# A differential-attention block on one core: the first row tile's scores as two matmuls of 256 columns instead of four of 128, with the sum of the two partial products moved from the matmul accumulator to VectorE

## The chip, the core and the metric

The kernel runs on one core of a Trainium2 chip. The engines named below are TensorE (PE in the profile; PEld is its weight load), VectorE (DVE), ScalarE (ACT) and GpSimd (POOL); SP is a queue that only starts transfers. The metric is the time of one execution on the device, in microseconds. Before the change three runs gave a median of 676.17 us (675.97 to 676.85).

## The reference, cut to what matters

One layer over 512 tokens of width 1024. A combined projection gives q, k, v, a pooling input and two gates; differential attention and a causal pooling branch are gated, summed and projected; a squared-ReLU MLP follows. The change touches only the scores of the attention, computed for 8 heads, each with two components c of 64 dimensions, and in four blocks of 128 query rows:

```python
for i in range(S // Q_BLOCK):                 # 4 blocks of 128 rows
    q0 = i * Q_BLOCK
    kend = q0 + Q_BLOCK                       # block i sees the first (i+1)*128 keys
    qb = q[:, q0:kend]
    kb = k[:, :kend]
    vb = v[:, :kend]
    s = jnp.einsum('bqhcd,bkhcd->bhcqk', qb, kb).astype(jnp.float32)
    mask = jnp.arange(kend)[None, :] <= (q0 + jnp.arange(Q_BLOCK))[:, None]
    s = jnp.where(mask, s, -jnp.inf)
    p = jax.nn.softmax(s, axis=-1)
    w = p[:, :, 0] - lam * p[:, :, 1]
    outs.append(jnp.einsum('bhqk,bkhd->bqhd', w.astype(v.dtype), vb))
```

All of it is float32. The kernel keeps that precision by splitting each operand into a high part, rounded to the matmul's own type, and a low part, the remainder.

## The kernel before, in words

**Stages.** First the value projection (v); then the attention stage, in which the projections of q and k, the scores, the pooling and the gates of all heads are mixed; then the output projection (po); then the MLP with its up and down products (um, dm).

**One head.** `qk(h)` projects q and k, applies the rotation on VectorE (`rope`, lines 349 to 353) and splits the results. For component c the 64 dimensions of q stand twice in the 128 partitions of `qs[:, c]`: the high part on the component's own half, the low part on the other. `kz[:, c]` has the high part of k on the own half and zeros on the other, `ks[:, c]` has the low part on the own half and the high part on the other. So `qs*ks` gives high times low plus low times high, `qs*kz` gives high times high, and the two sum to the score. `kz` are two fixed tiles, `ks` comes from a pool of two. Lines 379, 381 and 382 (ScalarE, ScalarE, VectorE) write them.

**The scores.** `attn(h)` goes over the four row tiles i with N = (i+1)*128 keys. For each component it takes one of two PSUM banks (3 and 4, in turn) and runs two matmuls into it, line 394 with `ks` and line 395 with `kz`, the second accumulating. VectorE's line 396 then adds the mask, scales, clips and takes the row extreme in one instruction. ScalarE's line 400 is the exponential with its row sum. Lines 402 to 405 normalize and combine the two components; line 409 transposes the result on TensorE (matmuls of 128 columns, i+1 of them for tile i); lines 411 and 412 split the transposed weights into `wt`; line 417 multiplies by the values.

**What sets the order.** The program is written head by head, with filler projections (gates `ga`, `gp` and pooling `u`) between heads by the table LAG. The framework then orders the instructions of every engine anew, by a timeline that it computes for itself at build time from its own costs. Each engine runs its list strictly in that order, so an instruction whose input is late holds all that stand behind it. A change of one operation can thus move many others.

**Other engines around it.** GpSimd adds for the pooling windows (line 452, after line 444 has made `u`), for the norm of the attention output (426, 427) and for the gated output (481), and starts accumulating transfers for low weight parts (line 122).

## Time and profile before

| | |
|---|---|
| median of the runs | 676.17 us |
| span of the profiled execution | 675.2 us |
| what the median has beside the span | 1.0 us |
| mean granted clock of TensorE | 0.998 |
| TensorE busy | 665.3 us, 99% |
| VectorE busy | 529.1 us, 78% |
| ScalarE busy | 462.5 us, 68% |
| GpSimd busy | 123.0 us, 18% |

The page gives the profiled execution's span, from its first to its last instruction, and no other time of it. A row of the timeline has the start of an instruction (or of a merged run of equal ones), its duration, engine, line, operation and its tiles, output before input. TensorE's rows overlap, since a matmul starts before the one ahead of it has drained; what a matmul costs in a dense stream is therefore read from the distance between starts, not from its duration. In a tile's name the buffer number is left out, so `s` is any score tile and `t` any transposed one.

### The profile page before, as it was taken

How to read it: one execution, taken by the hardware profiler on the slowest of the kernel's cores; microseconds unless marked ns; L12 is line 12 of the kernel's file. 1: busy time of each engine (PE TensorE's matmuls, PEld its weight loads, DVE VectorE, ACT ScalarE, POOL GpSimd, SP SyncE). 2: the span in 40 equal slices, each digit the busy share in tenths (PEclk: the TensorE clock that was granted, in tenths of full speed). 3: DMA queues.
4: the chain of work that ended last, by engine and by line, in shares of the span. 5: the costliest groups of instructions: out<-in, count | busy, mean ns of one | idle time of the engine just before them, and what ended most of it. 6: DMA issues, size and time to landing. Idle time of an engine off the chain costs nothing.

```text
span 675.2 us, 9995 instructions
## 1 busy us (share of the span) xinstructions
PE 665.3 (99%) x3686; PEld 579.9 (86%) x3686; DVE 529.1 (78%) x879; ACT 462.5 (68%) x741; POOL 123.0 (18%) x137
## 2 busy tenths in 40 slices
PE   9999999999999999999999999999999999999995
PEld 7788888888888888888889988899889998899884
DVE  6955877799979986975478989667994599747995
ACT  8465587978887698883477975367753696356874
POOL 6201110132133212520201020202103021210120
PEclk9999999999999999999999999999999999999999
DMA  8526574435254364574964678676969579493863
GB/s 272 189 71 182 126 152 125 102 94 126 87 139 105 101 171 94 126 193 177 309 194 79 196 172 241 153 179 155 234 190 197 200 156 260 125 213 131 213 125 124
DMA packets 32880, 109.34 MB, mean 162 GB/s; under 512 B 4032, under 2 KB 4928, under 8 KB 32832
## 3 DMA queue, kind: packets, MB, share of 16 engines
q0 software_dynamic: 10656, 38.80, 32.4%
q1 hardware_dynamic: 21744, 69.38, 29.0%
q8 instruction: 29, 0.48, 0.3%
q10 hardware_dynamic: 432, 0.52, 0.2%
q14 instruction: 19, 0.16, 0.1%
HBM read 106.59 MB, written 2.10 MB: 161 GB/s over the span
## 4 chain that ended last, share of the span: by engine, by line
PE 86%; DMA 5%; issue 5%; DVE 1%; ACT 1%; SPq 0%; DVEq 0%; POOLq 0%
PE dm L838 7%; PE dm L840 7%; PE dm L841 7%; PE um L759 7%; PE um L764 7%; PE um L761 7%; DMA wga_uNone<-w_up 5%; PE o L417 2%; PE ga L132 2%; PE ga L131 2%; PE gp L135 2%; PE k L132 2%; PE gp L132 2%; PE gp L131 2%; PE k L131 2%
## 5 line engine op out<-in xcount | busy, mean ns | idle before, releaser
L840 PE MATMUL dm<-wh_dt,z 128*128 128x512 f32 (+1 forms) x128 | 49.5, 387 | 0.0
L841 PE MATMUL dm<-wl_dt,z 128*128 128x512 f32 (+1 forms) x128 | 49.4, 386 | 0.0
L838 PE MATMUL dm<-wh_dt,z 128*128 128x512 f32 (+1 forms) x128 | 49.0, 387 | 0.0
L759 PE MATMUL um<-gss,wh_ut 128*128 128x256 f32 x192 | 48.1, 284 | 0.1
L761 PE MATMUL um<-gss,wh_ut 128*128 128x256 f32 x192 | 48.1, 283 | 0.0
L400 ACT ACTIVATE p<-p,st 128x128 f32<-128x128 f32 (+3 forms) x64 | 35.8, 560 | 14.1 <-DVE st L396 13.8
L112 ACT CAST wh_ut<-wga_uNone 128x1024 fp32r<-128x1024 f32 x24 | 24.9, 1053 | 28.8 <-PE dm L840 19.2
L856 DVE TENSOR_TENSOR x<-x,dm 128x512 f32<-128x512 f32 x48 | 32.8, 687 | 14.1 <-PE dm L841 14.0
L670 POOL DMA_DIRECT2D wga_dNone<-w_dn x16 | 14.2, 887 | 151.8 <-DVE wl_dt L113 151.8
L113 DVE TENSOR_TENSOR wl_ut<-wga_uNone,wh_ut 128x1024 fp32r<-128x1024 f32 x24 | 29.0, 1224 | 12.5 <-ACT wh_ut L112 12.5
L112 ACT CAST wh_ub<-wr_u 128x1024 fp32r<-128x1024 f32 x24 | 25.1, 1051 | 19.0 <-PE um L761 10.1
L670 POOL DMA_DIRECT2D wga_uNone<-w_up x18 | 15.6, 867 | 120.9 <-DVE wl_ut L113 86.9
L840 PE MATMUL dm<-wh_db,z 128*128 128x512 f32 x96 | 37.2, 389 | 0.0
L841 PE MATMUL dm<-wl_db,z 128*128 128x512 f32 x96 | 37.2, 389 | 0.0
L759 PEld LDWEIGHTS um<-gss,wh_ut 128*128 128x128 f32 x192 | 36.8, 192 | 0.3 <-ACT rawz L776 0.3
L761 PEld LDWEIGHTS um<-gss,wh_ut 128*128 128x128 f32 x192 | 36.9, 192 | 0.0
L838 PE MATMUL dm<-wh_db,z 128*128 128x512 f32 x96 | 35.8, 390 | 0.0
L113 DVE TENSOR_TENSOR wl_ub<-wr_u,wh_ub 128x1024 fp32r<-128x1024 f32 x24 | 29.2, 1222 | 7.9 <-ACT wh_ub L112 7.9
L112 ACT CAST wh_dt<-wga_dNone 128x1024 fp32r<-128x1024 f32 x24 | 24.8, 1050 | 14.6 <-issue 4.1
L735 DVE TENSOR_TENSOR z<-rawz,z 128x1024 fp32r<-128x1024 f32 x28 | 33.7, 1225 | 0.9 <-ACT z L732 0.9
L396 DVE CUSTOM_DVE_ANT_0 p<-s,mask 128x128 f32<-128x128 f32 (+3 forms) x64 | 30.3, 485 | 3.4 <-PE s L395 3.3
L732 ACT CAST z<-rawz 128x1024 fp32r<-128x1024 f32 x28 | 28.7, 1048 | 6.0 <-DVE rawz L741 4.9
(324 smaller groups left out, 2222.9 us busy)
## 6 DMA issues: line engine op xcount, KB each, us to landing
wr_u<-w_up SPq DMA_DIRECT2D x24, 512.0 KB, 5.3
wr_d<-w_dn SPq DMA_DIRECT2D x24, 512.0 KB, 4.2
wga_uNone<-w_up POOLq DMA_DIRECT2D x18, 512.0 KB, 6.7
wga_dNone<-w_dn POOLq DMA_DIRECT2D x16, 512.0 KB, 5.8
wr_k<-w_in SPq DMA_DIRECT2D x8, 512.0 KB, 3.3
wr_ga<-w_in SPq DMA_DIRECT2D x8, 512.0 KB, 3.3
wr_gp<-w_in SPq DMA_DIRECT2D x8, 512.0 KB, 4.2
wl_ga<-w_in POOLq DMA_DIRECT2D x8, 512.0 KB, 5.5
```

The source lines that it names most:

```text
L112: ins = A.copy(out=hi[:, sl], in_=raw[:, sl])
L113: (eng or G).tensor_tensor(out=lo[:, sl], in0=raw[:, sl], in1=f(hi)[:, sl], op=ALU.subtract)
L131: T.matmul(acc, lhsT=hi[:, c], rhs=rh[:, k, :], start=k == 0, stop=False)
L132: T.matmul(acc, lhsT=hi[:, c], rhs=rl[k], start=False, stop=False)
L400: A.activation(out=pr[:, c, :N], in_=pr[:, c, :N], func=AF.Exp, scale=-1.0, bias=st[:, c : c + 1], accum_out=st[:, 2 + c : 3 + c])
L735: V.tensor_tensor(out=z[:, 1], in0=r, in1=f(z[:, 0]), op=ALU.subtract)
L759: m = T.matmul(a_, lhsT=hi[:, c], rhs=rh[:, k, :], start=p + k == 0 and onto is None, stop=False, skip_group_check=True)
L761: T.matmul(a_, lhsT=hi[:, c], rhs=rl[:, k, :], start=False, stop=False, skip_group_check=True)
L764: m = T.matmul(a_, lhsT=lo[:, c], rhs=rh[:, k, :], start=False, stop=k == 3, skip_group_check=True)
L838: m = T.matmul(a_, lhsT=zh, rhs=hi[:, sl], start=p == 0 and start, stop=False, skip_group_check=True)
L840: T.matmul(a_, lhsT=zl, rhs=hi[:, sl], start=False, stop=False, skip_group_check=True)
L841: end = T.matmul(a_, lhsT=zh, rhs=lo[:, sl], start=False, stop=p == 3, skip_group_check=True)
```

## The change: what it does

The two copies of k, `ks` and `kz`, become two halves of one tile `kk` of shape 128 x 2 x 2 x 512 (copy, component, key). For the first row tile (i = 0, 128 keys) one matmul per component streams both copies, 2 x 128 columns, so that the two partial products land side by side in one PSUM bank; both components share that bank, 512 columns in all. VectorE then adds the mask to the first partial product of both components (a new instruction, 128 x 2 x 128) and writes it to `pr`; the instruction that adds the mask in the other row tiles here takes the second partial product and `pr` in the mask's place. Row tiles 1 to 3 are as before. The score banks are taken seven times per head, not eight.

```diff
--- before.py
+++ after.py
@@ -361,15 +361,14 @@
 
     lo_, hi_ = slice(0, 64), slice(64, 128)
 
-    kzs = [cf.tile([P, 2, S], F32R, name=f"kz{i}") for i in range(2)]
-    for kz in kzs:
-        G.memset(f(kz)[hi_, 0, :], 0.0)
-        G.memset(f(kz)[lo_, 1, :], 0.0)
+    kks = [cf.tile([P, 2, 2, S], F32R, name=f"kk{i}") for i in range(2)]
+    for kk in kks:
+        G.memset(f(kk)[hi_, 1, 0, :], 0.0)
+        G.memset(f(kk)[lo_, 1, 1, :], 0.0)
 
     def qk(h):
         qs = tp.tile([P, 2, S], F32R, tag="qs", name=f"qs{h}", bufs=2)
-        ks = tp.tile([P, 2, S], F32R, tag="ks", name=f"ks{h}", bufs=2)
-        kz = kzs[h % 2]
+        ks, kz = (kks[h % 2][:, i] for i in range(2))
         q = rope(proj(h, f"q{h}", V) if h else q0, f"q{h}")
         for c, own, oth in ((0, lo_, hi_), (1, hi_, lo_)):
             A.copy(out=qs[own, c, :], in_=q[own])
@@ -380,21 +379,31 @@
         for c, own, oth in ((0, lo_, hi_), (1, hi_, lo_)):
             A.copy(out=ks[oth, c, :], in_=f(kz)[own, c, :])
             V.tensor_tensor(out=ks[own, c, :], in0=k[own], in1=f(kz)[own, c, :], op=ALU.subtract)
-        return qs, ks, kz
-
-    def attn(h, qs, ks, kz):
+        return qs, kks[h % 2]
+
+    def attn(h, qs, kk):
+        ks, kz = (kk[:, i] for i in range(2))
         wt = wt_all
         for i in range(NT):
             N = (i + 1) * P
             qsl = slice(i * P, i * P + P)
             pr = tmp(f"p{i}", f"p{h}_{i}", (P, 2, N), bufs=1)
             st = tmp("st", f"st{h}_{i}", (P, 6), bufs=3)
+            if i == 0:
+
+                both = sbk(f"s{h}_0").rearrange("p (c k n) -> p c k n", c=2, k=2)
+                for c in range(2):
+                    T.matmul(both[:, c], lhsT=qs[:, c, qsl], rhs=kk[:, :, c, :P], start=c == 0, stop=True, skip_group_check=True)
+                diag = mask[:, S - P :].rearrange("p (o n) -> p o n", o=1).to_broadcast([P, 2, P])
+                V.tensor_tensor(out=pr, in0=both[:, :, 0], in1=diag, op=ALU.add)
             for c in range(2):
-                s_ = sbk(f"s{h}_{i}_{c}")
-                T.matmul(s_[:, :N], lhsT=qs[:, c, qsl], rhs=ks[:, c, :N], start=True, stop=False)
-                T.matmul(s_[:, :N], lhsT=qs[:, c, qsl], rhs=kz[:, c, :N], start=False, stop=True)
+                if i:
+                    s_ = sbk(f"s{h}_{i}_{c}")
+                    T.matmul(s_[:, :N], lhsT=qs[:, c, qsl], rhs=ks[:, c, :N], start=True, stop=False)
+                    T.matmul(s_[:, :N], lhsT=qs[:, c, qsl], rhs=kz[:, c, :N], start=False, stop=True)
                 V.tensor_tensor_reduce(
-                    out=pr[:, c, :N], in0=s_[:, :N], in1=mask[:, S - N :], scale=-0.125, scalar=-NEG,
+                    out=pr[:, c, :N], in0=s_[:, :N] if i else both[:, c, 1], in1=mask[:, S - N :] if i else pr[:, c],
+                    scale=-0.125, scalar=-NEG,
                     op0=ALU.add, op1=ALU.min, accum_out=st[:, c : c + 1],
                 )
                 A.activation(out=pr[:, c, :N], in_=pr[:, c, :N], func=AF.Exp, scale=-1.0,
```

In the changed kernel the score matmuls are lines 396 (first tile), 402 and 403; the new VectorE addition is line 398, the mask and extreme line 404, the combination line 414, the split of the transposed weights line 421; line 382 has become 381, line 444 line 453, line 435 line 444, line 409 line 418.

**The order on TensorE, head 0, first row tile.** In the rows, `s0_0` and `s0_1_0` are score tiles (head, row tile, component, then a buffer number), `ga0` a gate projection that runs between them. Before:

```order
L131 MATMUL ga0_893<-xh_84,wh_ga0_888 128x512
L394 MATMUL s0_0_0_635<-ks0_579,qs0_578 128x128
L395 MATMUL s0_0_0_635<-kz0_572,qs0_578 128x128
L132 MATMUL ga0_893<-xlb_86,wh_ga0_888 128x512
L394 MATMUL s0_0_1_640<-ks0_579,qs0_578 128x128
L395 MATMUL s0_0_1_640<-kz0_572,qs0_578 128x128
```

Now:

```order
L131 MATMUL ga0_889<-xh_84,wh_ga0_884 128x512
L396 MATMUL s0_0_634<-kk0_572,qs0_578 128x256
L402 MATMUL s0_1_0_652<-kk0_572,qs0_578 128x256
L403 MATMUL s0_1_0_652<-kk0_572,qs0_578 128x256
L396 MATMUL s0_0_634<-kk0_572,qs0_578 128x256
L132 MATMUL ga0_889<-xlb_86,wh_ga0_884 128x512
```

Four rows of 128 columns have become two of 256, and the first scores of row tile 1 stand between them.

**The order on VectorE, head 0, the same place.** `p0_0` and `p0_1` are the masked scores of row tiles 0 and 1, `st` their row extremes. Before:

```order
L353 TENSOR_TENSOR q1k1_824<-q1k1_824,swk1_826 128x512
L396 ISA p0_0_633,st0_0_634<-s0_0_0_635,mask_96 128x128
L396 ISA st0_0_634 128x1
L456 SCALAR_TENSOR_TENSOR pb0_873<-pa0_872,u0_869 128x512
L396 ISA p0_0_633,st0_0_634<-s0_0_1_640,mask_96 128x128
```

Now:

```order
L353 TENSOR_TENSOR q1k1_820<-q1k1_820,swk1_822 128x512
L398 TENSOR_TENSOR p0_0_632<-s0_0_634,mask_96 128x256
L465 SCALAR_TENSOR_TENSOR pb0_869<-pa0_868,u0_865 128x512
L404 ISA p0_0_632,st0_0_633<-s0_0_634,p0_0_632 128x128
L404 ISA st0_0_633 128x1
```

One addition of 256 elements per partition stands ahead of the two instructions that were there already.

**The order around the last transpose of head 4.** First VectorE, up to the combination `p4_3` that this transpose reads; `kk1` holds the k of head 5, `u2` starts the pooling adds of GpSimd, `o3` and `y3` belong to the output norm of head 3. Before (the combination of `p4_2`, row tile 2, stands eleven rows ahead of the first of these):

```order
L403 TENSOR_SCALAR st4_3_1915<-st4_3_1915,lvec_506 128x1
L444 TENSOR_TENSOR u2_2087<-u2_2062,rb_114 128x512
L435 SCALAR_TENSOR_TENSOR o3_1628<-o3_1628,con_73,y3_1639 128x512
L382 TENSOR_TENSOR ks5_1969<-q1k5_2042,kz1_573 64x512 x2
L405 SCALAR_TENSOR_TENSOR p4_3_1914<-p4_3_1914,st4_3_1915 128x512
```

Now:

```order
L414 SCALAR_TENSOR_TENSOR p4_2_1877<-p4_2_1877,st4_2_1878 128x384
L205 SCALAR_TENSOR_TENSOR sqo3_1621<-ss3_1624,sqo3_1621 128x512
L353 TENSOR_TENSOR q1k5_2026<-q1k5_2026,swk5_2028 128x512
L421 TENSOR_TENSOR wt_571<-t4_1_1872,wt_571 128x2x128
L411 RECIPROCAL st4_3_1900<-st4_3_1900 128x2
L453 TENSOR_TENSOR u2_2071<-u2_2046,rb_114 128x512
L206 SCALAR_TENSOR_TENSOR y3_1627<-sqo3_1621,y3_1627 128x512
L412 TENSOR_SCALAR st4_3_1900<-st4_3_1900,lvec_506 128x1
L381 TENSOR_TENSOR kk1_573<-q1k5_2026,kk1_573 64x512 x2
L444 SCALAR_TENSOR_TENSOR o3_1616<-o3_1616,con_73,y3_1627 128x512
L414 SCALAR_TENSOR_TENSOR p4_3_1899<-p4_3_1899,st4_3_1900 128x512
```

The two combinations have come nearer to each other, and `u2` now stands ahead of line 206. On TensorE the transposes `t4_2` and `t4_3` that read them have come nearer too. Before, 32 matmuls of 512 columns and two of 128 stood between them; now these rows, with seven matmuls of `ga4` and seven of `q6`, each of 512 columns, between `t4_2` and the first of them:

```order
L396 MATMUL s5_0_2127<-kk1_573,qs5_1953 128x256
L402 MATMUL s5_1_0_2145<-kk1_573,qs5_1953 128x256
L403 MATMUL s5_1_0_2145<-kk1_573,qs5_1953 128x256
L132 MATMUL q6_2247<-xla_85,wh_q6_2243 128x512
L396 MATMUL s5_0_2127<-kk1_573,qs5_1953 128x256
L131 MATMUL q6_2247<-xh_84,wh_q6_2243 128x512
```

Four more rows of `q6` follow, and then `t4_3`. Between the two transposes there are now 20 matmuls of 512 columns and four of 256. Past the attention stage the lists of all engines are as before, and SP's list is as before throughout.

## The prediction

> **What bounds the kernel now.** I read the page first, for the shares of the engines and the chain of work that ended last; then the waits of TensorE; then the busy time in four stretches of the attention stage, in which the change lies.
>
> ```profile
> PE 665.3 (99%) x3686; PEld 579.9 (86%) x3686; DVE 529.1 (78%) x879; ACT 462.5 (68%) x741; POOL 123.0 (18%) x137
> PE 86%; DMA 5%; issue 5%; DVE 1%; ACT 1%; SPq 0%; DVEq 0%; POOLq 0%
> ```
>
> ```profile
> PE h2T L629 <- ACT h2f L646: 0.6, 1, 0.6
> PE um L759 <- ACT gss L602: 0.3, 1, 0.3
> ```
>
> TensorE is busy for 99% of the span and makes up 86% of the chain. A busy row of TensorE includes its drain, so the share alone is no proof; but apart from the start, the waits that the profile finds for it are these two, both behind the attention stage, and two more of 0.3 us or less ahead of it. In the attention stage no matmul waits by this view. So time saved in TensorE's stream there is time saved at the end, unless another engine becomes late. VectorE is the next one:
>
> ```profile
> 166.00:194.00 28.00, 28.00 (x136) 23.36 (x136) 23.02 (x49) 22.81 (x38) 6.75 (x6) 1.00 0.45 113
> 194.00:222.00 28.00, 28.00 (x136) 23.18 (x135) 27.59 (x56) 21.43 (x44) 10.79 (x10) 1.00 0.38 102
> 222.00:253.00 31.00, 31.00 (x152) 26.00 (x151) 27.63 (x69) 24.17 (x50) 6.06 (x6) 1.00 0.52 131
> ```
>
> The columns are the stretch, its length, then the busy time of PE, PEld, DVE, ACT and POOL, the clock and the DMA share. VectorE has 5.0 us of idle time between 166 and 194 us (28.00 - 23.02) and 3.4 us between 222 and 253 us, but only 0.4 us between 194 and 222 us, where heads 4 and 5 meet. The granted clock is 1.00 in all, so a duration read in one place holds in another.
>
> **What the change takes from TensorE.** Eight heads times four matmuls of 128 columns go, eight times two of 256 come; the number of streamed columns is the same. What each costs is read from distances between starts (first the 128-column scores of head 0, then 256-column scores a little later):
>
> ```profile
> 81.71 0.39 PE L131 MATMUL ga<-xh,wh_ga 128*128 128x512 f32 x1
> 81.94 0.22 PE L394 MATMUL s<-ks,qs 128*128 128x128 f32 x1
> 82.00 0.27 PE L395 MATMUL s<-kz,qs 128*128 128x128 f32 x1
> 82.11 0.45 PE L132 MATMUL ga<-xlb,wh_ga 128*128 128x512 f32 x1
> 82.39 0.22 PE L394 MATMUL s<-ks,qs 128*128 128x128 f32 x1
> 82.45 0.28 PE L395 MATMUL s<-kz,qs 128*128 128x128 f32 x1
> 82.56 0.45 PE L131 MATMUL ga<-xh,wh_ga 128*128 128x512 f32 x1
> 82.85 0.40 PE L132 MATMUL ga<-xlb,wh_ga 128*128 128x512 f32 x1
> ```
>
> ```profile
> 86.95 0.39 PE L132 MATMUL q<-xla,wh_q 128*128 128x512 f32 x1
> 87.17 0.28 PE L394 MATMUL s<-ks,qs 128*128 128x256 f32 x1
> 87.29 0.28 PE L395 MATMUL s<-kz,qs 128*128 128x256 f32 x1
> 87.41 0.39 PE L131 MATMUL q<-xh,wh_q 128*128 128x512 f32 x1
> 87.64 0.28 PE L394 MATMUL s<-ks,qs 128*128 128x256 f32 x1
> 87.75 0.28 PE L395 MATMUL s<-kz,qs 128*128 128x256 f32 x1
> 87.87 0.39 PE L132 MATMUL q<-xla,wh_q 128*128 128x512 f32 x1
> ```
>
> A 512-column matmul stands 0.227 us ahead of its successor where eight follow one another (1.81 us for eight in the chain: "PE q L135 x8"):
>
> ```profile
> 61.93 1.81 PE q L135 x8
> 380.93 0.48 PE um L764 x4
> ```
>
> From 81.71 to 82.85 us lie three matmuls of 512 columns and four of 128: 1.14 - 3*0.227 = 0.46 us, or 0.115 us for each of 128 columns. From 86.95 to 87.87 us lie two of 512 and four of 256: 0.92 - 2*0.227 = 0.47 us, or 0.117 us for each of 256; the second row of the last fence gives 0.120. So a matmul of 128 columns costs as much as one of 256: halving the columns saves nothing, since each has its own load of weights. The gain is 32*0.115 - 16*0.117 = 3.68 - 1.87 = **1.8 us**. Its bounds: if only the distance from 81.94 to 82.00 us counted, 0.06 us per 128 columns, 32 of them would be 1.9 us and the gain nothing; with 0.120 for 256 columns it is 1.76 us. I take 1.8, since the stretch that ends on a matmul of 512 columns contains what the short ones delay.
>
> The Trainium skill (TensorE: Matmul & The Clock Gate, section Back-to-back issue gap) gives about 81 ns per matmul and weight load at 128 columns. By that 32 of them would be 2.6 us and the gain an estimated 0.7 us, which would make the change hard to see; this trace has 115 ns, and the measurement decides.
>
> **What the change adds to VectorE.** One addition per head over 256 elements from PSUM and SBUF, eight in all. The nearest rows are the split of 256 transposed weights, which also reads one operand of each kind, and the masked score instruction, which stays twice per head:
>
> ```profile
> L412 DVE TENSOR_TENSOR wt<-t,wt 128x256 fp32r<-128x256 f32 x8 | 3.3, 417 | 1.3 <-ACT wt L411 1.3
> L396 DVE CUSTOM_DVE_ANT_0 p<-s,mask 128x128 f32<-128x128 f32 x16 | 4.3, 284 | 0.5 <-PE s L395 0.4
> ```
>
> So 0.42 us per head, 3.3 us in all. Its lower bound is a row of 128 elements, 0.28 us, its upper bound the 0.69 us that line 206 takes for 512 (below). Most of it lies in VectorE's idle time beside TensorE's stream: 5.0 us in the stretch of head 3, 3.4 us in that of heads 5 and 6. Without that cover all 3.3 us would stand on the path. The fewer bank turns (seven for eight) and the same zeroing of the tiles cost nothing that can be seen: both score banks are used as before, and the score matmuls that need a bank back stand microseconds behind its readers.
>
> **Where the addition is not covered: the last transpose of head 4.** These are VectorE, GpSimd and TensorE there, from the timeline:
>
> ```profile
> 205.49 0.62 DVE L405 SCALAR_TENSOR_TENSOR p<-p,st 128x384 f32<-128x384 f32 x1
> ...
> 208.98 0.49 PE L409 MATMUL t<-ident,p 128*128 128x128 f32 x3
> ...
> 209.57 0.69 DVE L206 SCALAR_TENSOR_TENSOR y<-sqo,y 128x512 f32<-128x512 f32 x1
> ...
> 210.91 0.74 DVE L435 SCALAR_TENSOR_TENSOR o<-o,con,y 128x512 f32<-128x512 f32 x1
> ...
> 211.07 1.48 POOL L452 TENSOR_TENSOR pa<-u 128x512 f32<-128x512 f32 x1 [10.85 <-DVE u L444]
> 211.57 3.23 DVE L382 TENSOR_TENSOR ks<-q1k,kz 64x512 fp32r<-64x512 f32 x2
> ...
> 212.51 1.74 POOL L481 TENSOR_TENSOR o<-o,g 128x512 f32<-128x512 f32 x1
> ...
> 214.81 1.34 POOL L452 TENSOR_TENSOR pb<-pa 128x512 f32<-128x512 f32 x1
> 214.83 1.88 DVE L405 SCALAR_TENSOR_TENSOR p<-p,st 128x512 f32<-128x512 f32 x1
> ...
> 216.86 0.63 PE L409 MATMUL t<-ident,p 128*128 128x128 f32 x4
> ```
>
> ```profile
> L382 DVE TENSOR_TENSOR ks<-q1k,kz x16: 676/690/1674, 76.4 to 263.5; 64x512 fp32r<-64x512 f32 x16
> ```
>
> The combination of row tile 2 ends at 206.11 us and its transpose starts 2.87 us later; that of row tile 3 ends at 216.71 us and its transpose starts 0.15 us later. There is the thinnest cover of the stage. The pair of line 382 took 3.23 us where two of its median are 1.38, while GpSimd ran its additions: a stretch of 1.85 us, and the row at 214.83 is stretched likewise (line 382's own minimum, median and maximum stand in the last row).
>
> In the new order 20 matmuls of 512 columns, four of 256 and the three blocks of the first transpose lie between the two transposes: 20*0.227 + 4*0.117 + 3*0.115 = 5.4 us. VectorE has eleven steps there: lines 205, 353, 421, 411, 453, 206, 412, 381 twice, 444 and 414. The pair of line 381 and line 414 as they stood are 3.23 + 1.88 = 5.1 us. The eight others are estimated from rows above: five of 512 elements at 0.7, one of 256 at 0.42, two small ones at 0.2, less some 0.1 of overlap at each (line 435 starts at 210.91, line 382 at 211.57, 0.08 before the first one's end), 3.5 us. Together 8.6 us. VectorE thus loses 8.6 - 5.4 = 3.2 us on TensorE from one transpose to the next. The lead of 2.87 us is shortened by head 4's addition (0.42) and by head 4's saving on TensorE (0.2) to 2.25. The transpose then waits **0.95 us**. Without stretches (1.38 and 0.7) the eleven steps are 5.6 us and nothing waits; that is the lower bound. I take 0.8, near the upper end, since `u2`, which starts GpSimd's additions, still stands just ahead of line 381. What is late next is the output of head 4 and the first tile of head 5; they follow in the same order, so the wait is paid once, and VectorE's idle time from 222 us on (3.4 us by the stretch above) makes it up.
>
> **The sum.** Made against the profiled execution: 675.2 - 1.8 + 0.8 = 674.2 us of span. The median of the runs was 1.0 us above that span, so **675.2 us**, 0.14% below 676.17.
>
> **The rivals.** A change of 0.2%, 1.35 us, is about what a measurement of this kernel can tell from none.
>
> *No new wait.* GpSimd's additions fall elsewhere, and the eleven steps take their 5.6 us. For it: the order was made anew with the addition in it, and the other transpose of the fence above stands 2.87 us behind what it reads. Against it: `u2` stands where it stood. Time: 676.2 - 1.8 = 674.4 us.
>
> *Slower: the collision grows.* With `u2` ahead of line 206, GpSimd's first addition (1.48 us) also meets line 206, and its second (1.74) line 444; held for their whole length these add 1.4 and 1.0 us to the 8.6, and the transpose waits 8.6 + 2.4 - 5.4 - 2.25 = 3.4 us. It decides from a wait of 3.15 us on (1.8 + 1.35). Time: 676.2 - 1.8 + 3.4 = 677.8 us. For it: the row at 211.57. Against it: line 435, which stood right behind `u` before, took 0.74 us and was not held.
>
> The Trainium skill (SBUF — State Buffer, section SBUF: two separate sides) says that a VectorE instruction with two SBUF inputs and a GpSimd instruction that reads SBUF exclude each other for a whole instruction. The stretches agree with it (3.23 for 1.38 us). By it the new addition, which reads PSUM, is safe, and lines 206 and 444 are not.
>
> *Given back at the MLP's entry.* The first up products wait for transfers that accumulate weights, which are on the chain there:
>
> ```profile
> 367.93 8.28 DMA wga_uNone<-w_up x2
> ```
>
> If these did not start earlier, the matmuls behind would wait longer by what was saved: 676.2 us. Against it: the chain ahead of that transfer runs back through buffers that TensorE's own progress frees.
>
> **How the numbers follow.** One wait of 0.3 to 1.8 us in the stretch of heads 4 and 5: 0.47, with 674.7 to 676.2 us as its own range. No new wait: 0.34. The collision grows: 0.13. Given back: 0.06. The range is 674.1 to 677.3 us: below it only a gain beyond 1.8 us, above it the worse half of the collision. Faster by over 0.2% needs less than 674.8 us: nearly all of the second case and a tenth of the first, 0.36. Slower needs more than 677.5 us: most of the third, 0.12. The same: 0.52.
>
> **What would show it.** In the profile of the changed kernel the 16 score matmuls of line 396 stand 0.115 to 0.12 us apart where two follow each other, and the 128-column rows of scores are gone: the gain. Line 398 shows eight instructions of about 0.42 us: the addition. TensorE's waits show a transpose (line 418) behind line 414 near 216 us by 0.3 to 1.8 us, with a stretched pair of line 381 just ahead: the wait; a gap of under 0.3 us there means the second case, of over 3 us the third. I am wrong if line 396 costs clearly more than 0.12 us, if line 398 is held up like line 381, or if the waits come up at another place of the stage, above all in heads 6 and 7, whose order has changed as well.

## The result and the profile after

Six runs of the changed kernel had a median of 679.51 us (678.03 to 681.54), six of the kernel before 676.2 us (675.73 to 676.85): a ratio of 1.0041 (95% interval 1.0028 to 1.0054). Forecast was 675.2 us, within 674.1 to 677.3; the time lies above the range. Two repetitions, both on chip 13, gave 1.0027 (1.0014 to 1.0040) and 1.0035 (1.0023 to 1.0048), so the kernel is slower by 0.3 to 0.4%. Slower by more than 0.2% had been given a chance of 0.12.

The page of the profiled execution of the changed kernel (678.23 us, span 676.5) still has TensorE at the top, but the chain of work that ended last now runs through VectorE and ScalarE for 9% of the span, where it was 2%:

```profile
PE 664.8 (98%) x3670; PEld 577.3 (85%) x3670; DVE 533.9 (79%) x887; ACT 459.7 (68%) x741; POOL 121.4 (18%) x137
PE 81%; DMA 5%; DVE 5%; ACT 4%; issue 3%; POOL 1%; SPq 0%; POOLq 0%; DVEq 0%
```

TensorE's waits (all those from the attention stage on) have a new first line, and the one at the MLP's entry is 0.7 us where it was 0.3:

```profile
PE t L418 <- DVE p L414: 0.9, 1, 0.9
PE um L768 <- ACT gss L611: 0.7, 1, 0.7
PE h2T L638 <- ACT h2f L655: 0.5, 1, 0.5
```

What the change was to do, it does. The timeline shows the merged matmuls 0.12 us ahead of their successors (81.86 to 81.97, 82.21 to 82.33), and the rows of the two new lines have 16 matmuls of 256 columns and eight additions of 0.41 us, none of them held up:

```profile
81.86 0.28 PE L396 MATMUL s<-kk,qs 128*128 128x256 f32 x1
81.97 0.29 PE L402 MATMUL s<-kk,qs 128*128 128x256 f32 x1
82.09 0.28 PE L403 MATMUL s<-kk,qs 128*128 128x256 f32 x1
82.21 0.28 PE L396 MATMUL s<-kk,qs 128*128 128x256 f32 x1
82.33 0.40 PE L132 MATMUL ga<-xlb,wh_ga 128*128 128x512 f32 x1
```

```profile
L396 PE MATMUL s<-kk,qs x16: 277/278/383, 81.9 to 264.2; 128*128 128x256 f32 x16
L398 DVE TENSOR_TENSOR p<-s,mask x8: 409/414/419, 83.0 to 266.9; 128x256 f32<-128x256 f32 x8
```

The span is cut here at five matmuls of TensorE whose start the traces give: the last of v, the last of o (the end of attention), the last transpose h2T, the last up product and the last down product. All times below are read in this way.

| profiled execution | start to last v | attention: to last o | to last h2T | MLP's up: to last um | to last dm | to the end | span |
|---|---|---|---|---|---|---|---|
| before | 57.01 | 248.16 | 55.48 | 268.80 | 36.82 | 8.89 | 675.17 |
| changed | 56.93 | 249.08 | 55.45 | 269.29 | 36.82 | 8.90 | 676.47 |

So the profiled execution lost 0.9 us in the attention stage, where a gain was expected, and 0.5 us behind it at the MLP's entry, where nothing was changed. The remaining columns differ by 0.1 us or less. The 0.5 us is a low reading: the kernel before repeats less well in that column (268.80 here; 268.18, 268.44 and 268.52 in e2, g1 and g2 below), the changed kernel well (269.25 to 269.34 in three profiles).

The largest new wait is in head 6. These are the rows around it, first of the kernel before, then of the changed one, from VectorE, GpSimd, ScalarE and TensorE:

```profile
260.40 0.69 DVE L353 TENSOR_TENSOR q1k<-q1k,swk 128x512 f32<-128x512 f32 x1
260.58 0.62 ACT L404 ACTIVATE p<-p,st 128x384 f32<-128x384 f32 x1 [1.02 <-DVE st L403]
261.63 0.61 DVE L405 SCALAR_TENSOR_TENSOR p<-p,st 128x384 f32<-128x384 f32 x1
264.71 0.49 PE L409 MATMUL t<-ident,p 128*128 128x128 f32 x3
```

```profile
258.35 1.11 POOL L435 TENSOR_TENSOR sqo<-o 128x512 f32<-128x512 f32 x1
258.42 1.60 DVE L353 TENSOR_TENSOR q1k<-q1k,swk 128x512 f32<-128x512 f32 x1
260.05 1.26 ACT L378 CAST kk<-q1k 64x512 fp32r<-64x512 f32 x2 [1.29 <-DVE q1k L353]
264.20 0.62 ACT L413 ACTIVATE p<-p,st 128x384 f32<-128x384 f32 x1
264.85 0.62 DVE L414 SCALAR_TENSOR_TENSOR p<-p,st 128x384 f32<-128x384 f32 x1 [1.78 <-ACT p L413]
265.52 0.55 PE L418 MATMUL t<-ident,p 128*128 128x128 f32 x3 [0.91 <-DVE p L414]
```

GpSimd began an addition 0.07 us ahead of VectorE's line 353; that line took 1.60 us where 0.68 to 0.69 is usual. ScalarE waited 1.29 us for it, did its casts of K and its exponentials one behind the other, and scaled row tile 2 only at 264.20; VectorE's combination and the transpose stand at the end of that chain. In the kernel before ScalarE scaled this tile ahead of the casts of K (261.12), so that line 353 was not in its chain, and the transpose stood 2.46 us behind the combination's end.

### The profile page after: what moved, and what is told of

Its sections match the earlier page's. It is cut to its first block, busy times and chain, and to the rows that moved or that the text cites. A ratio compares the mean times of both kernels' runs of the same rounds, so it can differ in the third digit from the quotient of the medians.

```text
span 676.5 us, 9966 instructions
## 1 busy us (share of the span) xinstructions
PE 664.8 (98%) x3670; PEld 577.3 (85%) x3670; DVE 533.9 (79%) x887; ACT 459.7 (68%) x741; POOL 121.4 (18%) x137
## 4 chain that ended last, share of the span: by engine, by line
PE 81%; DMA 5%; DVE 5%; ACT 4%; issue 3%; POOL 1%; SPq 0%; POOLq 0%; DVEq 0%
PE dm L847 7%; PE dm L849 7%; PE dm L850 7%; PE um L768 7%; PE um L773 7%; PE um L770 7%; DMA wga_uNone<-w_up 4%; PE gp L131 2%; PE gp L132 2%; PE gp L135 2%; PE v L236 2%; PE ga L131 2%; PE ga L132 2%; PE ga L135 2%; PE v L237 2%
## 5 line engine op out<-in xcount | busy, mean ns | idle before, releaser
L113 DVE TENSOR_TENSOR wl_dt<-wga_dNone,wh_dt 128x1024 fp32r<-128x1024 f32 x24 | 29.1, 1220 | 4.7 <-ACT wh_dt L112 4.6
L768 PE MATMUL um<-gab,wh_ub 128*128 128x256 f32 x128 | 32.5, 285 | 0.0
```

The lines of the kernel that those rows point to most:

```text
L113: (eng or G).tensor_tensor(out=lo[:, sl], in0=raw[:, sl], in1=f(hi)[:, sl], op=ALU.subtract)
L768: m = T.matmul(a_, lhsT=hi[:, c], rhs=rh[:, k, :], start=p + k == 0 and onto is None, stop=False, skip_group_check=True)
```

## The experiments

The kernels of one group (one letter) ran on one chip beside fresh runs of the kernel before, and one execution of each was profiled. The column "attention" is the stretch from the last matmul of v to the last of o. It repeats to 0.1 us for one order of work: 248.16 and 248.11 for the kernel before, 249.08, 249.04 and 249.10 for the changed kernel. The stretch to the last h2T, which the table leaves out, was 55.5 to 56.2 us, with a wait of TensorE for ScalarE of 0.5 to 1.3 us in it.

| run | median, us | before on that chip | ratio (95%) | start | attention | MLP's up | end |
|---|---|---|---|---|---|---|---|
| e1_again | 679.04 | 677.43 | 1.0027 (1.0014–1.0040) | 56.26 | 249.04 | 269.34 | 8.91 |
| e2_layout | 678.06 | 677.43 | 1.0013 (1.0001–1.0025) | 57.06 | 248.19 | 268.44 | 8.87 |
| e3_noadd | 677.39 | 677.43 | 0.9998 (0.9990–1.0007) | 56.99 | 246.64 | 269.30 | 8.88 |
| e4_hold62 | 680.92 | 677.43 | 1.0046 (1.0029–1.0064) | 55.95 | 249.25 | 269.13 | 9.76 |
| f1_pin_before | 679.86 | 676.99 | 1.0056 (1.0043–1.0068) | 58.24 | 248.40 | 269.30 | 9.76 |
| f2_noadd_order | 677.83 | 676.99 | 1.0011 (1.0002–1.0020) | 57.81 | 247.01 | 268.86 | 8.87 |
| f3_swap62 | 679.62 | 676.99 | 1.0043 (1.0030–1.0055) | 57.67 | 248.96 | 269.00 | 8.89 |
| f4_addonly_order | 679.65 | 676.99 | 1.0045 (1.0032–1.0059) | 57.97 | 249.01 | 268.56 | 9.79 |
| g1_before | 677.62 | 677.56 | 1.0002 (0.9993–1.0010) | 57.82 | 248.11 | 268.18 | 8.88 |
| g2_before_order | 677.06 | 677.56 | 0.9991 (0.9982–0.9999) | 57.66 | 248.08 | 268.52 | 8.87 |
| g3_mixed_order | 677.84 | 677.56 | 1.0009 (0.9996–1.0022) | 57.79 | 248.01 | 268.46 | 8.88 |
| g4_pin_again | 680.22 | 677.56 | 1.0042 (1.0029–1.0055) | 58.51 | 248.44 | 269.42 | 9.76 |
| h1_after_fetch | 680.44 | 677.15 | 1.0046 (1.0028–1.0063) | 60.40 | 249.08 | 268.42 | 8.90 |
| h2_before_dve8 | 678.42 | 677.15 | 1.0017 (1.0009–1.0026) | 57.60 | 248.28 | 268.62 | 9.77 |
| h3_u2late_fetch | 680.96 | 677.15 | 1.0058 (1.0045–1.0071) | 61.21 | 247.82 | 268.33 | 8.88 |
| i1_after_fetch2 | 679.48 | 677.04 | 1.0041 (1.0026–1.0057) | 60.77 | 249.04 | 268.54 | 8.90 |
| i2_after | 679.34 | 677.04 | 1.0035 (1.0023–1.0048) | 57.36 | 249.10 | 269.25 | 8.89 |
| i3_best | 676.49 | 677.04 | 0.9996 (0.9986–1.0007) | 58.10 | 247.15 | 268.98 | 8.86 |

Two theories stood at the beginning. By the order theory the framework, which orders the instructions anew with each kernel, had merely drawn transposes too close to what they read. By the load theory VectorE has no room for 3.3 us more work in the places where it stands, in any order.

### First group: is the saving real, and what does the rest of the change do?

The changed kernel once more:

> The changed kernel once more, nothing altered, timed on the same chip as the three that follow, and profiled a second time. Order theory (the saving of 1.8 us is real, and the new order leaves transposes of the attention stage so close behind the exponentials and divisions they read that TensorE waits): 678 to 680 us again, the largest wait of the attention stage again at the transpose of head 6, row tile 2, near 265 us (0.9 us plus the cluster behind it, about 1.6 us over what the same place had before). Load theory (VectorE is simply short of time for 3.3 us more): the same time, but waits wherever VectorE is fullest, 194 to 222 us among them. If the time is back at 676 us, the first result was a chance of the chip.

The layout alone (`ks` and `kz` as halves of one tile kept for all heads, otherwise the code of before):

```diff
-        ks = tp.tile([P, 2, S], F32R, tag="ks", name=f"ks{h}", bufs=2)
-        kz = kzs[h % 2]
+        ks, kz = (kks[h % 2][:, i] for i in range(2))
```

> Only the new place of K: ks and kz as two halves of one tile that is kept for all heads, with the four matmuls of 128 columns and without the addition; the order of TensorE's work is that of before, row for row. Order theory and load theory: 676.2 us, as before (675.7 to 676.9). If the shared tile itself costs (a dependency between the halves, or a reuse of ks that comes too early), 678 us or more.

The changed kernel without its addition:

```diff
-                diag = mask[:, S - P :].rearrange("p (o n) -> p o n", o=1).to_broadcast([P, 2, P])
-                V.tensor_tensor(out=pr, in0=both[:, :, 0], in1=diag, op=ALU.add)
...
-                    ... in1=mask[:, S - N :] if i else pr[:, c],
+                    ... in1=mask[:, S - N :],
```

> The changed kernel without VectorE's addition: row tile 0 leaves out the partial product of ks, and the mask goes straight into the reduction, as before. TensorE keeps the 256-column matmuls. Saving real and the addition (with the order that follows from it) to blame: 674.4 us (676.2 - 1.8), up to 675.5 where the order still moves a transpose. Saving not real (the merged matmul costs what it takes away): 676.2 us or more. Reorder alone to blame, with no part of VectorE's load: 677 us or more.

One order dependency that puts the late transpose of head 6 behind a later matmul of `u3` (ahead of that transpose nothing moved; behind it the framework moved other rows of heads 6 and 7 too):

```diff
+HOLD = {"u3": ((6, 2), 4)}
...
+            if hold and k == hold[1]:
+                after(state[("t",) + hold[0]], m_)
```

> The changed kernel with one dependency of order alone: the transpose of head 6, row tile 2 is issued behind a matmul of u3 that is about 3.6 us later on TensorE; everything ahead of it keeps its place. Order theory: the wait there goes, and nothing takes its place at once, since VectorE has idle time behind it: 1.3 to 2 us less than the changed kernel of the same call. Load theory: VectorE is late anyway and the wait comes up at the next transposes (heads 6 and 7): the same time within 0.5 us.

The result repeats (679.04 us, 1.6 more than before). The tile costs nothing in the attention stage (248.19); in the whole time the run was 0.6 us slower, hardly clear of the noise (1.0001 to 1.0025), and why is open. Without the additions the stage takes 246.64 us, 1.5 less than before and 2.4 less than the changed kernel: TensorE's saving is real, and the additions take it back. The whole time of e3 does not show it: 677.39 us against 677.43, where 0.7 to 1.8 us less had been expected. Its MLP's up products took 269.30 us, 0.5 to 1.1 more than the kernel before, and each of its executions took 2.2 to 2.5 us beside its span, where the kernel before took 1.8 to 2.0; the first of these is followed up below, the second is open.

Holding the transpose did not help (249.25). The wait left the transpose, and the next tile's scores waited 1.5 us for a bank of VectorE's instead, since the same late combination stands ahead of the reduction that frees it:

```profile
PE s L406 <- DVE st L408: 1.5, 1, 1.5
```

This spoke against the order theory in its simple form: the wait had only been moved.

### Second group: order and load apart

To vary one of the two, the order was fixed. The kernels below end with a table of instruction numbers for each engine, and consecutive ones are tied by dependencies of order alone:

```diff
+        for one, two in zip(names, names[1:]):
+            tc.add_manual_dep(made[two], one, <NoSync>, reason="issue order")
```

> The whole change (merged matmuls, shared tile, addition), but every engine's instructions held to the order of the kernel before, by dependencies of order alone: each pair of 256 columns stands where the second of the two 128-column matmuls stood, each addition right ahead of the first masked reduction of its head. Order theory: the saving of 1.8 us comes through but for one wait of about 0.5 us at the last transpose of head 4 (its lead of 0.15 us loses 0.42 to the addition and 0.22 to TensorE's saving): a span of 673.9 us, 674.9 us or 1.3 less than before. Load theory: VectorE is late with 3.3 us more work in any order: waits of 2.5 us come up again and the time is 677 to 679 us.

> The changed kernel without the eight additions (row tile 0 leaves out the partial product of ks), all engines held to the changed kernel's own order. Order theory: the wait at the transpose of head 6, row tile 2 stays (0.7 to 0.9 us, since no addition lies between the stretched addition of line 353 and that transpose), and the time is 677 to 678 us, clearly above the version without additions in its own order. Load theory: without the 3.3 us the waits go, 674.5 to 675.5 us.

> The changed kernel held to its own order on all engines but for two places around head 6, row tile 2: ScalarE scales that tile's second component ahead of the exponential of row tile 3 and of the last cast of K, and VectorE takes the reciprocal and its product ahead of the second subtraction of K. No work is added or removed. Order theory: the tile is ready about 1.4 us earlier, the wait of 0.9 us at its transpose goes, and the kernel gains 0.9 to 1.6 us on the changed kernel (span of 675.0 to 675.5 us). Load theory: the wait moves to the next transposes or scores, the gain is below 0.4 us.

> The kernel before, in its own order on all engines, with one dead addition of 256 elements from PSUM and SBUF per head ahead of the first masked reduction (written where the reductions then write): the load alone, eight instructions of 0.42 us. Order theory: all but one lie in VectorE's idle time; 0.3 us of wait at the last transpose of head 4, so 676.2 to 676.7 us. Load theory: 2 to 3.3 us more than before, 678.2 to 679.5 us.

In the attention stage f2 and f3 went as the load theory had said, while f1 and f4 fell between the two. The dead addition alone, in before's own order, lengthened the stage by 0.9 us (249.01), where one theory had put 0 to 0.5 and the other 2 to 3.3. Its waits are two, both in heads 4 and 5:

```profile
PE t L412 <- DVE p L408: 0.3, 1, 0.3
PE s L394 <- DVE st L399: 0.2, 1, 0.2
```

The whole change in before's order (248.40) shows saving and loss one behind the other. Laid beside the kernel before, matmul by matmul, TensorE gains 0.21 us per head and is 0.83 us ahead near the end of head 3. It loses some 0.3 us there at the first matmuls of a projection, and 1.1 us at the last transpose of head 4:

```profile
212.77 1.48 POOL L461 TENSOR_TENSOR pa<-u 128x512 f32<-128x512 f32 x1 [10.85 <-DVE u L453]
213.26 3.23 DVE L381 TENSOR_TENSOR kk<-q1k,kk 64x512 fp32r<-64x512 f32 x2
216.53 1.88 DVE L414 SCALAR_TENSOR_TENSOR p<-p,st 128x512 f32<-128x512 f32 x1
218.55 0.63 PE L418 MATMUL t<-ident,p 128*128 128x128 f32 x4 [0.98 <-DVE p L414]
```

At that point VectorE sets the time. What TensorE had saved ahead of it is worth nothing, since VectorE comes no earlier, and each addition comes on top.

In the changed kernel's order the additions cost 2.1 us (249.08 against 247.01), and the order itself 0.4 (247.01 against 246.64 for the same work in an order of its own). The order theory had expected the wait in head 6 to stay without the additions. It went. (The whole time of f2, 677.83 us or 0.84 more than before, is the one that the order theory had forecast, but its loss lies outside the attention stage: that stage is 1.1 us shorter than before.) The rows say why the wait went:

```profile
258.13 0.68 DVE L353 TENSOR_TENSOR q1k<-q1k,swk 128x512 f32<-128x512 f32 x1
258.15 1.56 POOL L433 TENSOR_TENSOR sqo<-o 128x512 f32<-128x512 f32 x1
```

Here line 353 begins 0.02 us ahead of GpSimd and takes its 0.68 us; GpSimd's addition takes 1.56 us instead of 1.11. In the changed kernel it began 0.07 us behind GpSimd and took 1.60. The Trainium skill (SBUF — State Buffer, section SBUF: two separate sides) states that whichever starts first holds the port that the two share for its whole instruction; these two pairs of rows agree with it. A shift of a tenth of a microsecond, from additions that each look harmless, thus cost 0.9 us of VectorE's time and 1.2 us of TensorE's.

The swap in head 6 took the wait at 265 us away, and TensorE was 1.3 us ahead of the changed kernel; 1.15 us of that came back at the first transpose of head 7, behind the next collision:

```profile
281.35 1.58 POOL L461 TENSOR_TENSOR pb<-pa 128x512 f32<-128x512 f32 x1
281.51 1.58 DVE L414 SCALAR_TENSOR_TENSOR p<-p,st 128x128 f32<-128x128 f32 x1
283.23 0.30 PE L418 MATMUL t<-ident,p 128*128 128x128 f32 x1 [1.00 <-DVE p L414]
```

A combination of 128 columns, 0.35 us where nothing holds it, took 1.58 us here. In the changed kernel it had taken 1.60 us too, but the wait in head 6 had hidden it. So VectorE, ScalarE and GpSimd together are late through heads 6 and 7, and a swap only chooses where TensorE waits for them.

One thing fitted neither theory. f1 and f4 were 2.9 and 2.7 us slower than before, of which the attention stage holds 0.2 to 0.3 and 0.9.

### Third group: controls, and where the rest is

> The kernel before, unaltered, profiled a second time: how far its parts repeat. Both theories: the stretch from the last matmul of v to the last of o is 248.2 us again, as in the first profile and with the new tile alone (248.16 and 248.19); the stretch ahead of it (57.0), the end behind the last product (8.9) and the MLP's entry may differ, since they wait for transfers. If the part ahead is 57.8 to 58.2 us and the end 9.8, as in the kernels held to an order, these differences belong to the chip and the execution, not to a kernel.

> The kernel before with every engine held to its own order by the same kind of dependencies as in the experiments above: what the holding itself costs. If nothing: the time of the kernel before within 0.3 us, 248.2 us from the last matmul of v to the last of o. If holding costs by itself (waits that it brings, or its place in the program): up to 2 us more, ahead of and behind that stretch.

For the next one the diff to the held version of the change is a list of heads, `MERGED = (0, 1, 2, 6)`, outside of which the code of before stands:

> Before's order on all engines; heads 0, 1, 2 and 6 have the merged matmuls and the addition, heads 3, 4, 5 and 7 the four matmuls of 128 columns. Load theory, as it now stands (the addition costs nothing where VectorE has idle time and its whole length at the last transpose of head 4, where VectorE sets the time): the saving of three heads, 0.21 us each, is lost at that transpose, and at most head 6 keeps its 0.2: 248.0 us from the last matmul of v to the last of o, 676 us in all. Order theory: all four heads keep their saving, 247.3 us, 675.3 in all.

> The whole change in before's order once more, on the chip of the three runs above. Both theories: 248.4 us from the last matmul of v to the last of o, as in the first such run. If the whole time is again 2.9 us above before while that stretch is only 0.2 us longer, 2.7 us lie outside the attention stage: in the start (58.2 us against 57.0), the MLP's entry (0.5) and the end (9.8 against 8.9), and repeat with this kernel. If it is within 1 us of before, they were of that chip.

Fixing an order costs nothing (248.08 us of attention, 677.06 in all). The mixed version took 248.01 us, which the load theory had put at 248.0: the saving of heads 0 to 2 is gone behind head 4's last transpose, though head 4 itself was not changed, and head 6 keeps 0.2. In all it took 677.84 us against 677.56, where 676 had been expected.

The repetition of f1 was 2.7 us slower than before again, 0.3 of it in the attention stage. Against g1 and g2 on the same chip it lost 0.9 us or more in the MLP's up products, 0.9 at the end and 0.7 to 0.9 at the start.

Two of these three lie where a packet of instructions does. The profile's list of queues has two that carry instructions; the rows are packets, MB and share of 16 engines:

```profile
q8 instruction: 29, 0.48, 0.3%
q14 instruction: 19, 0.16, 0.1%
```

Queue 8 brings 29 packets of 16 KB for TensorE's 2 x 3686 matmuls and weight loads of the kernel before, about 254 instructions to a packet. The Trainium skill (Runtime: NRT & Kernel Launch, section Instruction fetch mechanics) gives blocks of 16 KiB with 256 instructions, which agrees, and says that the cost of crossing a block's boundary is mostly hidden. The cost seen here is another one, to transfers of the kernel itself.

The change takes 32 instructions from TensorE, so each later packet comes some 16 matmuls later. In the kernel before one came at 360.12 us, 0.5 us ahead of the last h2T; in the changed kernel it came at 365.42, 4.0 us behind it. These are the queue's rows in the stretch from 360.0 to 361.4 us of the one and from 365.2 to 366.6 of the other:

```profile
q8 instruction: 1, 0.02, 5.3%
```

```profile
q0 software_dynamic: 79, 0.27, 104.5%
q8 instruction: 1, 0.02, 4.4%
```
 
In the changed kernel it lies within the second accumulating transfer of weights for the MLP (queue 0), which is issued 1.1 us behind the first in both. This is when ScalarE could begin on the two transfers, before and changed:

```profile
365.33 1.05 ACT L112 CAST wh_ut<-wga_uNone 128x1024 fp32r<-128x1024 f32 x1 [1.76 <-DMA wga_uNone<-w_up]
367.81 1.05 ACT L112 CAST wh_ut<-wga_uNone 128x1024 fp32r<-128x1024 f32 x1 [0.39 <-DMA wga_uNone<-w_up]
```

```profile
366.06 1.05 ACT L112 CAST wh_ut<-wga_uNone 128x1024 fp32r<-128x1024 f32 x1 [1.69 <-DMA wga_uNone<-w_up]
369.33 1.05 ACT L112 CAST wh_ut<-wga_uNone 128x1024 fp32r<-128x1024 f32 x1 [1.18 <-DMA wga_uNone<-w_up]
```

The second cast follows the first by 2.48 us before and by 3.27 after; the packet itself takes 0.98 us. Over all 20 profiles of this document, those of the last two groups included: where the packet comes 3.5 to 4.1 us behind the last h2T (nine profiles), the second cast begins 7.45 to 8.03 us behind it; where the packet comes between 0.5 us ahead and 0.3 behind (eleven), it begins at 6.80 to 7.23, but for i3 with 7.55.

The end has a like pattern on queue 14. In the four profiles with 1090 VectorE instructions, semaphore and register instructions counted (e4, f1, f4, g4), a packet of 8 KB comes 3.0 us ahead of the end, and the last transfer of the output takes 3.7 us; in the others so far it comes behind the end or not at all, and that transfer takes 2.8 us.

### Fourth group: the packets moved on purpose

```diff
-    for _ in range(8):
+    for _ in range(6):
         T.matmul(warm[:, :P], lhsT=ones, rhs=ones, start=True, stop=True)
+    for _ in range(20):
+        T.matmul(warm[:, :16], lhsT=onesr, rhs=onesr[:, :16], start=True, stop=True)
```

> The changed kernel, held to its own order, with 16 more TensorE matmuls and weight loads among the warming ones at the start (six of 128 columns in fp32 and twenty of 16 columns in fp32r, where there were eight of 128): the same number of TensorE instructions ahead of the attention stage's end as the kernel before has. Instruction theory: a packet of 16 KB on queue 8, which carries instructions, lies inside the second accumulating weight transfer of the MLP's entry in the kernels with all heads merged, and ahead of it in the others; here it goes back ahead, that transfer lands 0.7 us earlier, and the part from the last h2T to the last up product falls from 269.3 to 268.5 us. If the packet has nothing to do with it: 269.3 us again. The attention stage stays at 249.1 us by both.

```diff
+    idle = cp.tile([P, 1], F32, name="idle")
+    for _ in range(8):
+        V.memset(idle, 0.0)
```

> The kernel before, in the same order, with eight dead VectorE memsets of one column at the start, where VectorE waits for its first data. Instruction theory: with eight more VectorE instructions a packet of 8 KB on queue 14 is fetched about 3 us ahead of the end, as in the four profiles with 1090 VectorE instructions, beside the last transfer of the output, which then takes 3.7 us instead of 2.8: 9.8 us from the last down product to the end (8.9 before), 0.9 us more in all. If the count of instructions is not the cause: 8.9 us and the time of the kernel before.

> The whole change in before's order with two alterations. First, the multiplication that starts GpSimd's additions of the third window (u2) stands behind the combination of head 4's row tile 3 instead of ahead of the subtractions of K, and what follows from it moves behind the first tile of head 5. Second, the warming matmuls as in the run above, and 24 dead VectorE memsets at the start. Load theory in its form with the collision (VectorE is late at head 4 because two subtractions of K and a combination are stretched by 3 us while GpSimd adds): the wait of 1.1 us there goes, 247.2 us from the last matmul of v to the last of o; with 268.5 at the MLP's entry and 8.9 at the end, 1.0 to 1.3 us less than the kernel before. If the load alone decides: a wait of 0.5 to 1 us at head 5 instead, 248 us or more.

Both packets did what was expected of them. With the dead matmuls TensorE's packet came at 364.98 us, 0.4 ahead of the last h2T; the second cast followed the first by 2.56 us, and the MLP's up products took 268.42 us:

```profile
369.82 1.05 ACT L112 CAST wh_ut<-wga_uNone 128x1024 fp32r<-128x1024 f32 x1 [1.55 <-DMA wga_uNone<-w_up]
372.38 1.05 ACT L112 CAST wh_ut<-wga_uNone 128x1024 fp32r<-128x1024 f32 x1 [0.47 <-DMA wga_uNone<-w_up]
```

The whole time did not fall, since the start took 3 us longer with the dead matmuls in it (60.40 us). And eight memsets of one column put into the kernel before, at its start, made its end 0.9 us longer, as forecast. The rows are the issue of the last output transfer in g1_before and in h2_before_dve8, the last column its time to landing; and the packet in the stretch from 673.0 to 674.2 us of the latter, 3 us ahead of its end:

```profile
out<-x ACTq DMA_DIRECT2D x1, 256.0 KB, 2.8
```

```profile
out<-x ACTq DMA_DIRECT2D x1, 256.0 KB, 3.7
q14 instruction: 1, 0.01, 1.6%
```

The whole kernel was 1.27 us slower for it (678.42 against 677.15; 1.0009 to 1.0026), 0.9 us of it at that place.

With `u2` moved behind the combination of head 4's last tile, that tile was not late any more. The pair of subtractions took 2.39 us and the combination 0.75, where they had taken 3.23 and 1.88:

```profile
215.62 2.39 DVE L386 TENSOR_TENSOR kk<-q1k,kk 64x512 fp32r<-64x512 f32 x2
218.06 0.75 DVE L419 SCALAR_TENSOR_TENSOR p<-p,st 128x512 f32<-128x512 f32 x1
```

TensorE was 0.9 us ahead of before at the end of head 4's product, and 0.35 ahead at the end: in head 5 some 0.7 us were lost, where score matmuls of row tiles 2 and 3 now waited for banks. The expectation of 247.2 us was met in part (247.82). Collision and load both count. The whole time, expected 1.0 to 1.3 us below before's, was 3.8 us above it, with the same dead matmuls in a start of 61.21 us.

### Fifth group: the start mended, and a version meant to beat both

```diff
+    dead = bank(6, "dead")
+    for _ in range(16):
+        T.matmul(dead[:, :16], lhsT=onesr, rhs=onesr[:, :16], start=True, stop=True)
```

> As h1, with the start mended: the eight warming matmuls as in the changed kernel, and sixteen dead matmuls of 16 columns put into a wait of TensorE near 21.5 us (0.3 to 0.7 us of idle time ahead of a matmul of v), since the twenty at the very start took 0.21 us each and delayed the start by 3 us. Instruction theory: 268.4 us from the last h2T to the last up product again, 249.1 us of attention stage, a start within 1 us of the changed kernel's; in all 0.3 to 0.8 us less than the changed kernel of the same call.

> The changed kernel itself, for the comparison with i1 on one chip: 249.1 us of attention stage, 269.3 us from the last h2T to the last up product, 8.9 us at the end; 1.5 to 2 us more than the kernel before.

```diff
+MERGED = (0, 1, 2, 4, 6, 7)
...
-            if i == 0:
+            one = i == 0 and h in MERGED
+            if one:
```

> A version meant to beat both: before's order, the change in heads 0, 1, 2, 4, 6 and 7 alone (the additions of heads 3 and 5 stood where VectorE was late), u2's window additions behind the combination of head 4's last tile, ten dead matmuls in the wait near 21.5 us and 24 dead memsets on VectorE at the start, so that both instruction packets lie where they hold up nothing. Load theory: 1.0 to 1.2 us less than before in the attention stage (247.0 to 247.2 us), 268.4 at the MLP's entry, 8.9 at the end; in all about 1 us less than before, ratio 0.9985. If the waits move on to heads 5 and 6 again: 247.8 us, and the time of before within 0.5 us.

By stage i1 confirms h1 (268.54 us against 269.25 of the changed kernel on the same chip). In the whole time it does not show: 679.48 against 679.34 us, where 0.3 to 0.8 less had been expected. The start of the profiled execution, expected within 1 us of the changed kernel's, was 3.4 us longer. The sixteen dead matmuls did not meet a wait there: they stood at 24.25 us and took 1.7. So the packet's share of the whole time is not shown by this pair. i3 has 247.15 us of attention, as the load theory forecast (247.0 to 247.2), 1.0 us less than before. In all it reached 676.49 against 677.04 us, with a ratio of 0.9996 (0.9986 to 1.0007): level with before, not better. Its packet came 0.3 us ahead of the last h2T, yet the MLP's up products took 268.98 us. Here it was the first of the two transfers that landed late: the first cast began 5.08 us behind the last h2T, and 4.27 to 4.67 in all the others. The packet took 1.33 us, the longest of all, and that transfer was already under way (issued 0.83 us ahead of the last h2T). That the packet held it up is not shown, since in f4 the packet lay 0.2 us ahead of the last h2T without such a delay (4.61).

## Why the prediction was wrong

**The gain on TensorE: right.** 1.8 us was forecast. The merged matmuls stand 0.12 us apart, and f1 shows 0.21 us per head, 1.7 us for eight. The 0.7 us estimated from the figure of the Trainium skill (TensorE: Matmul & The Clock Gate, section Back-to-back issue gap) was too low. The most of it that any kernel kept was 1.5 us, without the additions.

**The additions' own cost: right** (0.42 us each, 3.3 us in all, none held up).

**"Most of it lies in VectorE's idle time beside TensorE's stream": wrong, and this is the step that failed.** The prediction counted 5.0 and 3.4 us of idle time per stretch and took them for cover. They are sums over some 30 us. VectorE's rows stand in a fixed order and wait for ScalarE, for TensorE, and for GpSimd's hold on the port; idle time behind such a wait covers nothing ahead of it. In the changed kernel's order the additions cost 2.1 us of their 3.3, in before's order alone 0.9 us, and 0.2 to 0.3 us more than the whole saving together with it.

**One wait of 0.8 us at head 4's last transpose: the mechanism right, the place wrong for this order.** In before's order it came there as described, 1.1 us long, behind the stretched pair of K's subtractions (f1). In the changed kernel's order that transpose did not wait; it stood 1.12 us behind what it reads. TensorE took the 5.4 us between the two transposes that had been counted, but VectorE's eleven steps took 7.1 us and not 8.6, since GpSimd's additions stretched the pair of line 381 and not line 414 as well, and the lead they started from was 2.87 us and not 2.25:

```profile
211.91 2.86 DVE L381 TENSOR_TENSOR kk<-q1k,kk 64x512 fp32r<-64x512 f32 x2
215.47 0.74 DVE L414 SCALAR_TENSOR_TENSOR p<-p,st 128x512 f32<-128x512 f32 x1
```

The order had moved seven transposes to within 0.3 us of what they read (heads 2, 3, 5, 6 and 7; before it was this one alone). The waits came up there: beside the additions' own loss in heads 3 and 5 (about 0.4 us each against the same order without them) above all in head 6, where, by the prediction's last sentence, they would show it to be wrong. The prediction had counted the lead of one transpose in the new order, and not that of the others.

**"So the wait is paid once, and VectorE's idle time from 222 us on makes it up": wrong.** In f3 and h3, where one wait was taken away, most of the gain came back one or two heads later.

**The rival without a new wait (674.4 us, 0.34)** is refuted by the same rows.

**The rival of the growing collision (677.8 us, 0.13)** had the cause right, GpSimd holding VectorE, and the wrong place: not lines 206 and 444 in head 4 but line 353 and line 414 in heads 6 and 7 (1.60 us each, for 0.68 and 0.35). It was given too small a chance because only the place where the trace of before showed a collision was searched.

**The rival of the MLP's entry (676.2 us, 0.06)** had a loss at the right place: 0.5 us in the profiled execution, 0.5 to 1.2 us by all profiles of the two kernels. Its reason was not the one given (transfers that do not start earlier) but a packet of instructions that comes later, since TensorE has fewer of them. No view that the prediction read had shown it.

**The sum.** 675.17 - 1.7 (TensorE's saving) + 2.6 (lost again in the attention stage: 0.92 + 1.7; by e3, f2 and the changed kernel 0.2 without additions, 0.4 by the order, 2.1 by the additions) + 0.5 (MLP's entry) - 0.1 (the rest) = 676.5 us, the span of the profiled execution; its time was 678.23 us, 1.7 above the span. The prediction had put 1.0 for this, the median of three runs less the span of another execution. Wherever time and span of one execution are both on record, the changed kernel's time is 1.7 to 1.8 us above its span and that of the kernel before 1.8 to 2.0, so this term was mis-sized too. The medians lie 0.2 to 1.3 us above the profiled executions of the changed kernel (679.51 for 678.23, 679.04 for 677.90, 679.34 for 679.15). Of the other runs only the span is on record: on chip 13 the median span of the changed kernel is 1.75 and 2.5 us above that of the kernel before, of which the attention stage and the MLP's entry hold 1.3 to 2.2 by the profiles. What remains is open. A candidate is the start, which differed by 2.6 us among the profiles even without dead matmuls in it (55.95 to 58.51).

**The test of no difference.** The prediction took 0.2% as what can be told. With five to twelve runs of a kernel the intervals were 0.08 to 0.18% to each side, so this held.

## What to carry to other kernels

Idle time of an engine over a stretch is not cover for new work on it: look for the rows at which the bounding engine reads that engine's result with a few tenths of a microsecond of lead, and add the new work to the chain that ends there; ahead of such a row a saving on the bounding engine is worth nothing either. Where the order of work is made anew with each edit, hold it fixed in an experiment, so that load and order can be told apart, and compare stages rather than whole times. And when a change alters the number of instructions, look where the instruction packets now fall among the transfers that something waits for.

## What the runs showed of the hardware that was not expected

An instruction packet delays transfers. A packet of 16 KB (0.9 to 1.0 us) within a weight transfer on which the chain runs made it land 0.7 to 0.9 us later, and moving it away with dead instructions alone took that back in two kernels (h1, i1). One of 8 KB (0.31 us) beside the last transfer of the output made the end 0.9 us longer in the five profiles in which it lay there, one of them made on purpose (h2). Why 0.31 us cost 0.9 is not shown, nor why the first transfer of i3 was late.

Which of GpSimd and VectorE begins first, by 0.02 or 0.07 us, decides which of the two is stretched by 0.5 to 0.9 us.

The start has two speeds. The first matmuls of v begin 0.43 us apart in some profiles and 0.23 in others, and how many stand 0.43 us apart differs: none in the changed kernel, e1 and i2, eight in f1, ten in g4, eleven in h3. Here are the starts of the changed kernel, of i2 and of f1:

```profile
4.93 1.19 PE L235 MATMUL v<-wh_v,xh 128*128 128x512 f32 x4 [0.23 <-ACT wh_v L112]
5.96 0.40 PE L236 MATMUL v<-wl_v,xh 128*128 128x512 f32 x1
```

```profile
5.30 1.19 PE L235 MATMUL v<-wh_v,xh 128*128 128x512 f32 x4 [0.63 <-ACT wh_v L112]
```

```profile
5.69 2.07 PE L235 MATMUL v<-wh_v,xh 128*128 128x512 f32 x4 [0.77 <-ACT wh_v L112]
7.56 0.63 PE L236 MATMUL v<-wl_v,xh 128*128 128x512 f32 x1
7.99 0.63 PE L237 MATMUL v<-wh_v,xla 128*128 128x512 f32 x1
```

From the first matmul of v to the eleventh f1 took 4.3 us and the changed kernel 2.4. The start of f1 was 1.3 us longer in all (58.24 us against 56.93), since later waits for data took part of it back. The wait ahead of the first matmul of v does not decide it: f1 waited 0.77 us and had eight distances of 0.43 us, i2 waited 0.63 and had none, h3 did not wait at all and had the most. The granted clock in the profile is 1.00 there in f1 as in the changed kernel, so the cause is not shown. The Trainium skill (TensorE: Matmul & The Clock Gate, section Part 1: The HAM clock gate) describes an array clock that runs at half speed until the array has been busy for some 3.4 us, counted in a window that runs freely, so that the number of matmuls at half speed varies from run to run. The two distances and the varying number agree with that; the granted clock of 1.00 does not show it.
